# Two kernel tables issued by ScalarE, one embedding tile ahead of the first inner product, one weight split moved

## The chip, the cores and the metric

The kernel runs on one core of one Trainium2 chip. The metric is the device time in microseconds of one execution. The kernel before took 1217.81 us (median of three runs, 1214.92 to 1218.32). All matrix work is float32 done as three products of split halves, so TensorE (PE) is busy almost throughout; the change concerns one stage of about 60 us in the middle, where it is not.

## The reference, cut to what matters

Two layers over 512 positions of 1024 channels. Layer 0 mixes positions with a gated MLP and an attention, layer 1 with a diagonal complex state-space layer. After the mixing, each layer runs a gated feed-forward block and adds a gated embedding:

```python
for i in range(DEPTH):
    h = rms_norm(x, norm_mix[i])
    if i % 2 == 0:
        ...
    else:
        y = s5_mixer(h, ...)                     # 64 groups of 16 channels, 64 complex states each
        g_a, g_b = jnp.split(jax.nn.gelu(y) @ od_w_glu[o], 2, axis=-1)
        x = x + g_a * jax.nn.sigmoid(g_b)
    x = x + conv_ffn(rms_norm(x, norm_ffn[i]), ...)
    gate = jax.nn.sigmoid(rms_norm(x) @ ple_w_gate[i])
    x = x + gate * (p[i] @ ple_w_proj[i])
```

## The kernel before

The activations lie transposed, as eight tiles `x[0]` to `x[7]` of 128 channels by 512 positions. A product `W @ x` takes each weight chunk (128 x 1024 floats, 512 KB) as `raw` from HBM, splits it into a rounded part `whi` (ACT, line 136) and a remainder `wlo` (DVE, line 140), and does three matmuls per 128x128 block: `whi` with the low half of the activations (line 188), `whi` with the high half (189), `wlo` with the high half (190).

`Stream` (called `ws`) hands out the chunks in a fixed order. `n_dma`, `n_prep` and `n_use` count the chunks loaded, split and used; `prep(upto)` splits every chunk below `upto` that isn't split yet, but none at or beyond `limit`; `next()` first splits the chunk it hands out, if that has not been done, and then up to two more. There are four `raw` buffers and three of `whi` and `wlo`. Around the change the order of chunks is: eight of layer 0's gate (`w_gate`), two of layer 1's embedding projection (`w_proj`), sixteen of the GLU (`w_glu`).

The order of the instructions on each engine is that in which the Python code writes them; nothing reorders them. `after(n, fn)` puts a step off to a later `tick()`. `ple(0)` computes the gated embedding of layer 0; `gate(m)` and `add(m)` update `x[m]`, square it (`sq_add`) and write it, regrouped, to HBM (`s5_turn`) for the next stage.

`state_space` is the state-space layer. Its channels go in four rounds `b` = 0 to 3, two tiles each. For a round:

- `inputs(b)` (PE, line 1510) multiplies the regrouped activations `u` with input matrices `wv` into `V`.
- `frame(b)` (DVE, lines 1522 to 1533; one product, line 1526, on POOL) turns `V` by phase tables `tab`, scans along the sequence, and turns back; `states(b)` (DVE, line 1545) writes the states into `sg`.
- `inside(b)` (PE, line 1553) multiplies `u` with the kernel table `tt`, and `outside(b)` (PE, line 1562) adds the states times the output matrices `wo`, both into `Y`; ACT applies GELU to `Y` (line 1566).
- `turn(b)` transposes the result on PE (line 1575), and `done(b)` splits it into `ygh` (ACT, line 1590) and `ygl` (DVE, line 1591).

`tt`, `tab` and `wo` have two buffers each, and `wv` four. `load_kernel(b)` fills a `tt` with eight transfers of 128 KB, each for 16 partitions and in pieces of 512 bytes. All these loads stand in one queue, that of SP; each waits for its buffer to come free, and what stands behind it waits with it. One `tab` buffer, and the `sg` buffers, first hold the split embedding `phl` that `p_proj(w, m, ...)` multiplies by `w_proj` (lines 188 to 190, result `pk`), so `tab` of round 1 and the first write to `sg` wait for the last `p_proj`. `part` multiplies the GLU weights with what is ready of `yg`, and fills PE's time in rounds 2 and 3.

Of the kernel before, what the change touches and what calls it, by code (L numbers as in the profile page):

```python
# [19 lines left out]
P = 128  # L20
# [134 lines left out]
class Kern:  # L155
# [861 lines left out]
    def ple(self, layer, pl):  # L1017
        nc = self.nc
        pp = [pl.tile([P, T], F32, name=f"pp{m}") for m in range(KT)]
        self.after(1 + (layer == 0), self.rms_stat)  # L1020
        self.after(2 + (layer == 0), self.rms_bcast)
        if layer == 0:
            self.p_proj(lambda m, ps: nc.scalar.activation(pp[m], ps, AF.Copy))
        else:
            for m in range(KT):
                nc.sync.dma_start(pp[m], self.pd[m])

        gt = {}

        def gate(m, ps, c=slice(0, T)):  # L1030
            last = layer == 0 and m == KT - 1
            if c.start == 0:
                gt[m] = pl.tile([P, T], F32, name="gt", tag="gt", bufs=4)
            if last:
                add(m - 1)
            t = gt[m]
            nc.vector.tensor_tensor(t[:, c], ps[:, c], self.rB[:, c], ALU.mult)

            def rest():
                nc.scalar.activation(t[:, c], t[:, c], AF.Sigmoid)  # L1040
                if 0 < m < KT - 1 and c.start == 0:
                    add(m - 1)
                if m == KT - 1 or (layer and m == KT - 2):
                    add(m, c)

            self.post.append(rest)
            if m == KT - 1:
                self.run_post()

        def add(m, c=slice(0, T)):  # L1050
            t = gt[m]
            nc.vector.tensor_tensor(t[:, c], t[:, c], pp[m][:, c], ALU.mult)
            nc.vector.tensor_tensor(self.x[m][:, c], self.x[m][:, c], t[:, c], ALU.add)
            if layer == 0:
                if m == KT - 1:
                    self.s5_turn(m - 1, pl)
                self.sq_add(m, self.x[m], m == KT - 1)
                if m != KT - 2:
                    self.s5_turn(m, pl)
            else:  # L1060
                nc.sync.dma_start(self.out[m][:, c], self.x[m][:, c])

        for m in range(KT):
            hi, lo = self.ws.next()
            if layer and m == KT - 1:

                for c in (slice(0, T // 2), slice(T // 2, T)):
                    ps = self.acc()
                    xs = [(h[:, c], l[:, c]) for h, l in self.xh]
                    self.mtile(ps[:, c], hi, lo, range(KT), xs)  # L1070
                    gate(m, ps, c)
                continue
            ps = self.acc()
            self.mtile(ps, hi, lo, range(KT), self.xh)
            lag = 2 if layer and m < 2 else 1
            self.after(lag, lambda m=m, ps=ps: gate(m, ps))
            if layer == 0:
                self.s5_early(m)
            self.tick()
        if layer:  # L1080
            self.flush()
# [309 lines left out]
            self.nc.sync.dma_start(tab.rearrange("p a b -> p (a b)"), self.tabd[b])  # L1391
            self.units["tab", b] = tab[:, 0], tab[:, 1], self.de[b].rearrange("p g j -> p (g j)")

    def load_kernel(self, b):
        if b < 4:
            tt = self.s5a.tile([P, 16, P], F32, name="tt", tag="tt", bufs=2)
            src = self.kd[b].rearrange("(g c) k -> c g k", c=16)
            for i in range(8):
                self.nc.sync.dma_start(tt[i:P:8], src[:, :, P - 16 * i:2 * P - 16 * i])
            self.units["tt", b] = tt  # L1400

    def load_in(self, u):
# [59 lines left out]
    def state_space(self, s5b):  # L1462
        nc, gp, s5a = self.nc, self.gp, self.s5a

        def bank(b, name):
            return self.pp.tile([P, T], F32, name=name, tag=f"bank{b}", bufs=1)
# [4 lines left out]
        def p_proj(w, m, b):  # L1471
            ps = bank(b, "pk")
            o = 2 * (m % 4) * P
            self.mtile(ps, w[0][:, o:], w[1][:, o:], range(2), self.p)
            if m < 6:
                t = gp.tile([P, T], F32, name="pk", tag=("xh0", "xh1", "xh2", "xh3", "xl6", "xl7")[m])
            else:
                t = s5b.tile([P, T], F32, name="pk", tag=("ygh1", "ygl1")[m - 6], bufs=1)
            nc.scalar.activation(t, ps, AF.Copy)
            kept.append(t)  # L1480
# [19 lines left out]
        def inputs(b, b0, tiles=(0, 1)):  # L1500

            if 0 in tiles:
                V[b] = [bank(b0 + r, "V") for r in range(2)]
            vs = V[b]
            for uu in tiles:
                wv = self.units["wv", 2 * b + uu]
                for q in range(4):
                    for r in range(2):
                        for h in range(2):
                            nc.tensor.matmul(vs[r][64 * h:64 * h + 64, (4 * uu + q) * 64:(4 * uu + q + 1) * 64],  # L1510
                                             wv[:, r, q, 64 * h:64 * h + 64], self.ut[2 * b + uu][:, 2 * q + h],
                                             start=True, stop=True)
# [34 lines left out]
        def inside(b, b0):  # L1547

            Y[b] = [bank(b0 + z, "Y") for z in range(2)]
            tt = self.units["tt", b]  # L1550
            for g in range(8):
                for k in range(2):
                    nc.tensor.matmul(Y[b][g // 4][64 * k:64 * k + 64, g % 4 * P:(g % 4 + 1) * P],
                                     self.ut[2 * b + k][:, g], tt[:, 8 * k + g], start=g % 4 == 0, stop=False)
# [49 lines left out]
        w = self.ws.next()  # L1604
# [14 lines left out]
        w = self.ws.next()  # L1619
# [13 lines left out]
        for k in range(4, 8):  # L1633
            scaled(k, rt)
        self.ws.limit = None
        self.ws.prep(self.ws.n_use + 1)
        inside(0, 0)
        self.load_kernel(2)
        p_proj(w, 7, 7)
        inputs(1, 4)  # L1640
        self.load_in(6)
        self.load_in(7)
# [2 lines left out]
        outside(0)  # L1645
        self.load_out(2)
        self.load_out(3)
        self.load_kernel(3)
        for m in (6, 7):
            nc.sync.dma_start(self.pd[m], kept[m])  # L1650
        frame(1)
# [20 lines left out]
        w = self.ws.next()  # L1672
# [14 lines left out]
        w = self.ws.next()  # L1687
# [4 lines left out]
        w = self.ws.next()  # L1692
# [4 lines left out]
        w = self.ws.next()  # L1697
        for m in range(4):
            part(w, 2 * m, m, 4, 6)
        w = self.ws.next()  # L1700
# [14 lines left out]
        w = self.ws.next()  # L1715
# [35 lines left out]
```

## Time and profile before

| | before |
|---|---|
| median of three runs | 1217.81 us (1214.92 to 1218.32) |
| the profiled execution | 1216.31 us, span 1214.4 us |
| TensorE clock granted, mean | 0.995 |
| busy over the span: PE, PE weight loads, DVE, ACT, POOL | 98%, 80%, 65%, 44%, 21% |
| HBM read and written | 131.20 MB, 17.84 MB |

The profiled execution took 1.91 us more than its span. PE's share is an average: it is close to 100% before and after the state-space stage. That stage lies between 651 us (the first `p_proj`) and 725 us of the span; inside it the rows of the timeline, not the averages, tell what waits for what.

### The profile page before, as it was taken

What the parts mean: (1) busy time and instruction counts of PE and PEld (TensorE: products, weight loads), DVE (VectorE), ACT (ScalarE), POOL (GpSimd) and SP (SyncE); (2) the same over time, 40 slices, a digit from 0 to 9 for tenths busy, and PEclk for the clock granted to TensorE, in tenths of its full rate; (3) what the DMA queues carried; (4) which work ended last, traced back from release to release, by engine and by line L of the source; (5) the groups of instructions that cost most, each with busy time, mean ns of one, the idle gap of its engine ahead of it and who ended that gap; (6) DMA issues with size and microseconds to landing.
All of it is one profiled execution on the core that took longest, in us unless ns stands there. A gap on an engine that the chain in (4) does not pass through costs nothing. (4 is left out here: it accounts for less than half of the span.)

```text
span 1214.4 us, 15570 instructions
## 1 busy us (share of the span) xinstructions
PE 1191.8 (98%) x5858; PEld 966.7 (80%) x5858; DVE 784.2 (65%) x1160; ACT 531.5 (44%) x796; POOL 260.4 (21%) x440
## 2 busy tenths in 40 slices
PE   9999999999999999999999789999999999999998
PEld 7887678888888888887888678888888888888787
DVE  5696556599778776775546974449866532456545
ACT  6554664355444333444555224335534421344341
POOL 1652335860960221012302100110000000000110
PEclk9999999999999999999999989999999999999999
DMA  7223124233443545334487952322332333331441
GB/s 253 90 87 140 36 70 139 87 113 104 139 127 103 171 150 163 109 94 145 138 262 206 275 194 86 106 87 87 104 104 87 92 91 99 101 100 54 125 156 70
DMA packets 62314, 150.05 MB, mean 124 GB/s; under 512 B 14408, under 2 KB 23880, under 8 KB 62112
## 3 DMA queue, kind: packets, MB, share of 16 engines
q1 hardware_dynamic: 57504, 135.30, 35.9%
q0 software_dynamic: 4160, 12.90, 3.1%
q8 instruction: 46, 0.75, 0.3%
q10 hardware_dynamic: 576, 0.86, 0.2%
q14 instruction: 28, 0.23, 0.1%
HBM read 131.20 MB, written 17.84 MB: 123 GB/s over the span
## 5 line engine op out<-in xcount | busy, mean ns | idle before, releaser
L140 DVE TENSOR_TENSOR wlo<-raw,whi 128x1024 fp32r<-128x1024 f32 (+3 forms) x207 | 250.0, 1209 | 226.3 <-ACT whi L136 221.2
L136 ACT ACTIVATE whi<-raw 128x1024 fp32r<-128x1024 f32 (+3 forms) x207 | 209.0, 1011 | 354.2 <-PE acc L189 300.0
L188 PE MATMUL acc<-nl,whi 128*128 128x512 f32 x480 | 187.4, 390 | 0.0
L189 PE MATMUL acc<-nh,whi 128*128 128x512 f32 x480 | 187.0, 390 | 0.0
L190 PE MATMUL acc<-nh,wlo 128*128 128x512 f32 x480 | 187.0, 390 | 0.0
L241 POOL TENSOR_TENSOR sqa<-sqa,sqt 128x512 f32<-128x512 f32 x30 | 39.4, 1315 | 492.5 <-ACT sqt L237 492.4
L188 PE MATMUL acc<-xl,whi 128*128 128x512 f32 (+1 forms) x360 | 141.3, 392 | 0.0
L190 PE MATMUL acc<-xh,wlo 128*128 128x512 f32 (+1 forms) x360 | 140.5, 390 | 0.0
L189 PE MATMUL acc<-xh,whi 128*128 128x512 f32 (+1 forms) x360 | 140.5, 390 | 0.0
L188 PE MATMUL acc<-al,whi 128*128 128x512 f32 x352 | 139.2, 395 | 0.4 <-ACT whi L136 0.4
L190 PE MATMUL acc<-ah,wlo 128*128 128x512 f32 x352 | 138.0, 392 | 1.1 <-DVE wlo L140 1.1
L189 PE MATMUL acc<-ah,whi 128*128 128x512 f32 x352 | 137.8, 392 | 0.0
L188 PEld LDWEIGHTS acc<-nl,whi 128*128 128x128 f32 x480 | 90.2, 188 | 19.1 <-issue 0.4
L190 PEld LDWEIGHTS acc<-nh,wlo 128*128 128x128 f32 x480 | 90.1, 188 | 18.7
L189 PEld LDWEIGHTS acc<-nh,whi 128*128 128x128 f32 x480 | 90.2, 188 | 18.5
L925 DVE SCALAR_TENSOR_TENSOR cv<-acc,vecs,cv 128x511 f32<-128x511 f32 x120 | 89.5, 746 | 2.1
L190 PEld LDWEIGHTS acc<-xh,wlo 128*128 128x128 f32 x360 | 67.8, 188 | 15.5
L189 PEld LDWEIGHTS acc<-xh,whi 128*128 128x128 f32 x360 | 67.8, 188 | 15.2
L188 PEld LDWEIGHTS acc<-xl,whi 128*128 128x128 f32 x360 | 67.8, 188 | 15.2
L190 PEld LDWEIGHTS acc<-ah,wlo 128*128 128x128 f32 x352 | 66.1, 188 | 16.5 <-DVE wlo L140 1.9
L188 PEld LDWEIGHTS acc<-al,whi 128*128 128x128 f32 x352 | 66.1, 188 | 16.4 <-ACT whi L136 1.4
L189 PEld LDWEIGHTS acc<-ah,whi 128*128 128x128 f32 x352 | 66.1, 188 | 14.0
(385 smaller groups left out, 1944.0 us busy)
## 6 DMA issues: line engine op xcount, KB each, us to landing
raw<-w_up SPq DMA_DIRECT2D x88, 512.0 KB, 3.5
raw<-w_down SPq DMA_DIRECT2D x26, 512.0 KB, 3.6
raw<-w_in SPq DMA_DIRECT2D x19, 512.0 KB, 3.5
raw<-w_down SPq DMA_DIRECT2D x22, 384.0 KB, 3.1
raw<-w_gate SPq DMA_DIRECT2D x16, 512.0 KB, 3.5
raw<-w_glu SPq DMA_DIRECT2D x16, 512.0 KB, 4.3
x<-xT SPq DMA_DIRECT2D x16, 256.0 KB, 4.5
raw<-w_out SPq DMA_DIRECT2D x8, 512.0 KB, 3.6
```

The source lines that it names most:

```text
L136: k.nc.scalar.activation(hi[:, :n], t[:, :n], AF.Copy)
L140: e.tensor_tensor(lo[:, :n], t[:, :n], hi[:, :n].bitcast(F32), ALU.subtract)
L188: mm(out, whi, xlo, start=start, stop=False)
L189: mm(out, whi, xhi, start=False, stop=False)
L190: mm(out, wlo, xhi, start=False, stop=stop)
L241: (e or (nc.vector if m == KT - 1 else nc.gpsimd)).tensor_tensor(self.sqa, self.sqa, t, ALU.add)
L925: nc.vector.scalar_tensor_tensor(t[:, k:T], h[:, 0:T - k], w[2 - k], t[:, k:T], ALU.mult, ALU.add)
```

## The change

Three edits:

1. `add(7)` in `ple(0)` calls `prep(n_use + 2)` between the regrouping of `x[6]` and the squaring of `x[7]`, with the limit lifted for the call. In `state_space` the call `prep(n_use + 1)` after `states(0)` is removed.
2. The last embedding tile `p_proj(w, 7, 7)` stands ahead of `inside(0)`; it stood behind.
3. The kernel tables of rounds 2 and 3 are issued from ACT's queue; they were issued from SP's.

```diff
@@ ple: add(m), layer 0
                 if m == KT - 1:
                     self.s5_turn(m - 1, pl)
+                    self.ws.limit = None
+                    self.ws.prep(self.ws.n_use + 2)
+                    self.ws.limit = self.ws.n_use + 2
                 self.sq_add(m, self.x[m], m == KT - 1)
@@ load_kernel
-    def load_kernel(self, b):
+    def load_kernel(self, b, q=None):
...
-                self.nc.sync.dma_start(tt[i:P:8], src[:, :, P - 16 * i:2 * P - 16 * i])
+                (q or self.nc.sync).dma_start(tt[i:P:8], src[:, :, P - 16 * i:2 * P - 16 * i])
@@ state_space
         self.ws.limit = None
-        self.ws.prep(self.ws.n_use + 1)
+        p_proj(w, 7, 7)
         inside(0, 0)
-        self.load_kernel(2)
-        p_proj(w, 7, 7)
+        self.load_kernel(2, nc.scalar)
         inputs(1, 4)
...
         self.load_out(3)
-        self.load_kernel(3)
+        self.load_kernel(3, nc.scalar)
```

The changed code has three lines more ahead of `state_space`, so a line of that function that is L1562 before is L1566 in the changed kernel.

What the change does to the order on ACT, from the squaring of the last tile `x_119` to the third round. Before (`xp` is the regrouped tile, `pk` an embedding tile, `kd_87` and `kd_88` are the tables of rounds 2 and 3 in HBM):

```order
L237 ACTIVATE sqt<-x_119 128x512
L1417 ACTIVATE xp<-x_119 128x512
L1479 ACTIVATE pk<-pk 128x512 x7
L136 ACTIVATE whi<-raw 128x1024
L1479 ACTIVATE pk<-pk 128x512
L1566 ACT_TABLE_LOAD
L1566 ACTIVATE y<-Y 128x4x8x16 x2
L1590 ACTIVATE ygh_6202<-Z 128x128x4 x2
L1566 ACTIVATE y<-Y 128x4x8x16 x2
L1590 ACTIVATE ygh_6355<-Z 128x128x4 x2
L136 ACTIVATE whi<-raw 128x1024 x2
```

The same stretch of ACT in the changed kernel:

```order
L237 ACTIVATE sqt<-x_119 128x512
L1421 ACTIVATE xp<-x_119 128x512
L1483 ACTIVATE pk<-pk 128x512 x8
L1403 DMA tt<-kd_87 16x16x128 x8
L1570 ACT_TABLE_LOAD
L1570 ACTIVATE y<-Y 128x4x8x16 x2
L1403 DMA tt<-kd_88 16x16x128 x8
L1594 ACTIVATE ygh_6198<-Z 128x128x4 x2
L1570 ACTIVATE y<-Y 128x4x8x16 x2
L1594 ACTIVATE ygh_6351<-Z 128x128x4 x2
L136 ACTIVATE whi<-raw 128x1024 x3
```

The sixteen table transfers stand around the first GELU, ahead of the first `ygh`. The split of the first GLU chunk has left its place among the `pk`; it does not stand by the squaring, but behind the second round's `ygh`, with the next two.

On DVE, the place where round 1's `frame` begins (`u_5907` is the last tile scaled, `V` what `frame(1)` reads), and the place ahead of round 3's `frame`. Before:

```order
L1496 TENSOR_TENSOR u_5907<-u_5907,rj 128x512
L140 TENSOR_TENSOR wlo<-raw,whi 128x1024
L1522 TENSOR_TENSOR st_6154<-V,tab 128x512
L1523 TENSOR_TENSOR st_6155<-V,tab 128x512
...
L1545 TENSOR_TENSOR sg_5859<-st_6311,st_6307 64x8x63 x2
L140 TENSOR_TENSOR wlo<-raw,whi 128x1024 x2
L1522 TENSOR_TENSOR st_6428<-V,tab 128x512
```

DVE in the changed kernel, from the last update of `x_119` to the reciprocal root `rc` of the summed squares, and then the same two places:

```order
L1053 TENSOR_TENSOR x_119<-x_119,gt 128x512
L254 TENSOR_SCALAR rc<-aux 128x4
...
L1500 TENSOR_TENSOR u_5907<-u_5907,rj 128x512
L1526 TENSOR_TENSOR st_6150<-V,tab 128x512
L1527 TENSOR_TENSOR st_6151<-V,tab 128x512
...
L1549 TENSOR_TENSOR sg_5859<-st_6307,st_6303 64x8x63 x2
L140 TENSOR_TENSOR wlo<-raw,whi 128x1024 x3
L1526 TENSOR_TENSOR st_6428<-V,tab 128x512
```

One `wlo` has moved from ahead of `frame(1)` to ahead of `frame(3)`, where there are now three in a row; between `x_119` and `rc` there is none. On PE only the six matmuls of the last `pk` have changed places with the 32 of `inside(0)`, and on SP the two tables are gone from between the other loads.

## The prediction

> **What bounds the kernel now.** I read the spans and the granted clock first, then busy time by stretch, then the timelines of DVE, PE, SP and ACT through the state-space stage. All times are of the profiled execution of before: 1216.31 us, span 1214.4 us. Its three other runs have a median of 1217.81 (1214.92 to 1218.32). The clock, then engine by engine the busy time of three stretches:
>
> ```profile
> core 0: 1214.4 us, clock 0.995
> ...
> 180.00:640.00 460.00, 459.28 (x2150) 374.56 (x2149) 325.88 (x421) 209.09 (x314) 162.84 (x278) 1.00 0.44 138
> 645.00:725.00 80.00, 67.44 (x699) 55.96 (x697) 66.90 (x91) 27.66 (x40) 10.72 (x10) 0.94 0.77 221
> 725.00:1210.00 485.00, 484.13 (x2150) 397.84 (x2148) 265.71 (x331) 184.07 (x241) 19.48 (x14) 1.00 0.31 97
> ```
>
> PE idles 0.72 us before the state-space stage, 12.56 us inside these 80 us, and 0.87 us behind them. So time can only be won or lost inside. DVE, where it says "<-" what ended an idle time:
>
> ```profile
> 657.24 0.16 DVE L254 TENSOR_SCALAR rc<-aux 128x4 f32<-128x4 f32 x1 [1.87 <-PE aux L245]
> ...
> 671.91 2.79 DVE L1545 TENSOR_TENSOR sg<-st,st 64x504 f32<-64x504 f32 x4
> 674.73 2.50 DVE L1496 TENSOR_TENSOR u<-u,rj 128x512 f32<-128x512 f32 x4
> 677.15 1.22 DVE L140 TENSOR_TENSOR wlo<-raw,whi 128x1024 fp32r<-128x1024 f32 x1
> 678.28 0.69 DVE L1522 TENSOR_TENSOR st<-V,tab 128x512 f32<-128x512 f32 x1
> ...
> 686.62 1.28 DVE L1591 TENSOR_TENSOR ygl<-Z,ygh 128x512 fp32r<-128x512 f32 x2
> 687.93 2.79 DVE L1545 TENSOR_TENSOR sg<-st,st 64x504 f32<-64x504 f32 x4
> ...
> 703.27 2.36 DVE L140 TENSOR_TENSOR wlo<-raw,whi 128x1024 fp32r<-128x1024 f32 x2
> 705.55 0.68 DVE L1522 TENSOR_TENSOR st<-V,tab 128x512 f32<-128x512 f32 x1
> ...
> 715.18 2.79 DVE L1545 TENSOR_TENSOR sg<-st,st 64x504 f32<-64x504 f32 x4
> ```
>
> No row of DVE from 663 to 719 us has an idle note, those shown among them: DVE runs without a gap, and the last `sg` (715.18 + 2.79 = 717.97) sets when PE can finish `outside(3)`. PE (start, duration, line, count, idle before):
>
> ```profile
> 665.56 1.97 PE L1553 MATMUL Y<-tt,u 128*64 128x128 f32 x32
> 667.46 0.50 PE L188 MATMUL pk<-phl,whi 128*128 128x512 f32 x1
> ...
> 674.76 1.75 PE L1562 MATMUL Y<-wo,sg 128*64 128x128 f32 x28 [0.18 <-DVE sg L1545]
> 680.52 3.58 PE L1553 MATMUL Y<-tt,u 128*64 128x128 f32 x32 [4.02 <-DMA wv<-wvd]
> 684.03 1.09 PE L1575 MATMUL Z<-ident,y 128*128 128x128 f32 x8
> ...
> 699.88 0.50 PE L188 MATMUL acc<-ygl,whi 128*128 128x512 f32 x1 [2.60 <-DVE ygl L1591]
> ...
> 705.81 1.97 PE L1562 MATMUL Y<-wo,sg 128*64 128x128 f32 x32
> ...
> 718.03 3.25 PE L1562 MATMUL Y<-wo,sg 128*64 128x128 f32 x28 [0.27 <-DVE sg L1545]
> 721.21 0.58 PE L188 MATMUL acc<-ygl,whi 128*128 128x512 f32 x1
> ```
>
> PE waits 4.02 us before `inside(2)` and 2.60 us before the first GLU `part`; from 721.21 it runs to the end. So the end of the kernel is the start of the row at 721.21 plus constant work. Clock by stretch (PEclk is the column behind the five engines):
>
> ```profile
> 680.50:684.10 3.60, 3.58 (x33) 3.37 (x34) 3.53 (x5) 0.00 (x0) 1.28 (x1) 0.53 1.02 404
> 701.00:704.30 3.30, 3.30 (x10) 2.52 (x9) 3.19 (x5) 0.00 (x0) 0.00 (x0) 0.50 0.06 26
> 717.80:721.20 3.40, 3.17 (x28) 2.85 (x28) 1.40 (x2) 0.60 (x1) 0.00 (x0) 0.53 0.27 54
> ...
> 699.88:715.63 15.75, 15.75 (x88) 12.57 (x88) 15.43 (x21) 3.23 (x5) 1.29 (x1) 0.89 0.69 242
> ```
>
> After a mostly idle stretch PE runs some 3.3 us at half clock: 32 matmuls of `inside(2)` take 3.58 us, 32 of `outside(2)` at 705.81 take 1.97. The third half-clock stretch hits `outside(3)` itself: its 28 matmuls take 3.25 us, the same form at 674.76 takes 1.75. That is 1.5 us on the path.
>
> **The split of the first GLU chunk.** It does not go where the change writes it. When `add(7)` runs, all eight gate chunks are used and nothing more, so `prep(n_use + 2)` asks for the two embedding chunks, which the `next()` of the last gate chunk has split already. The call does nothing, and the gap of 1.87 us before 657.24 stays empty. With the later `prep` removed, the chunk is split by the `next()` ahead of the first `part`: the order of the changed kernel has `whi` behind the second `ygh` and `wlo` behind `states(2)`. So:
>
> - ACT: one instruction of 1.05 us leaves a place where ACT had nothing else (row 666.21 below) and goes to one where ACT is idle too: 0 us. If that cover were gone, 1.05 us.
> - DVE: the row at 677.15 goes, and `frame(1)` starts 678.28 - 677.15 = 1.13 us earlier. It comes back behind 703.24: two take 2.36, three 3.49. At `frame(3)` the sum is 0.
> - PE: before, the first `part` waited only for its PSUM bank (`ygl` of round 1). Now its third matmul needs the moved `wlo`.
>
> **The embedding tile ahead of inside(0).** Six matmuls (1.4 us) and 32 (1.97 us) change places; `inputs(1)` starts when it did, so PE gains and loses nothing. But the tile's input lies in `sg`, which POOL clears before its product of frame 0:
>
> ```profile
> 668.49 0.19 POOL L1625 MEMSET sg<- 128x16 f32 x2 [9.99 <-PE pk L190]
> 668.67 1.47 POOL L1526 TENSOR_TENSOR st<-st,tab 128x512 f32<-128x512 f32 x1
> ```
>
> ```profile
> 669.09 1.59 DVE L1531 TENSOR_TENSOR st<-st,tab 128x512 f32<-128x512 f32 x1
> ...
> 684.80 0.69 DVE L1531 TENSOR_TENSOR st<-st,tab 128x512 f32<-128x512 f32 x1
> ```
>
> POOL's product overlaps DVE's L1531, which takes 1.59 us, where the same line takes 0.69 in round 1, at 684.80, clear of POOL. In the changed order the clearing comes about 2 us earlier, and the product ends before L1531; it will lie on L1529 instead and cost some of it. The loss is 1.59 - 0.69 = 0.9; I take a gain of 0.3, between 0 and 0.9, because most of it comes back at L1529. Together with the split, `frame(1)` starts 1.43 us earlier and ends near 685.2 instead of 686.6.
>
> **The tables.** SP and ACT:
>
> ```profile
> 669.14 0.32 SPq L1391 DMA_DIRECT2D tab<-tabd  x1
> 669.51 5.79 SPq L1399 DMA_DIRECT2D tt<-kd  x8
> 675.39 1.02 SPq L1405 DMA_DIRECT2D wv<-wvd  x2
> ...
> 678.70 9.65 SPq L1399 DMA_DIRECT2D tt<-kd  x8
> ```
>
> ```profile
> tt<-kd SPq DMA_DIRECT2D x2, 128.0 KB, 5.4
> ```
>
> ```profile
> 666.21 1.05 ACT L136 ACTIVATE whi<-raw 128x1024 fp32r<-128x1024 f32 x1
> ...
> 669.77 1.28 ACT L1566 ACT_TABLE_LOAD   x1
> 675.68 0.60 ACT L1566 ACTIVATE y<-Y 128x512 f32<-128x512 f32 x1 [4.63 <-PE Y L1562]
> ...
> 684.73 1.09 ACT L1590 ACTIVATE ygh<-Z 128x512 fp32r<-128x512 f32 x2 [7.55 <-PE Z L1575]
> ```
>
> The first is the queue of SP: a phase table, eight pieces of `tt` for round 2, then `wv` and, at 678.70, eight pieces for round 3. The last piece of round 2 was issued in the window 674.5 to 675.3 and took 5.4 us to land, so about 680.1 to 680.5, just when `inside(2)` starts: that wait, which the chain of waits lays on `wv`, is one for `tt`.
>
> Issued by ACT, they can start when `inside(0)` is done, now at the end of the embedding tile's old place, 669.05: 0.45 us earlier than 669.51. Eight issues at 5.79 / 8 = 0.72 us end at 674.9, the GELU's table load (1.28) at 676.2, the two GELUs at 677.5; before, the second ended at 677.2. So round 2's table costs ACT nothing that anybody waits for: `outside(0)` ends at 676.5 in any case, and PE reads this GELU only behind `inside(2)`. Round 3's eight issues follow, and behind them on ACT is `ygh` of round 0, for which DVE waits with `ygl` and everything after. At 0.72 us each they end at 683.3, at the 9.65 / 8 = 1.21 us of row 678.70 at 687.2. DVE would want `ygl` at 685.2, about 0.6 us behind the first `ygh`; so the stall is 0 to 2.6 us, and between the two, at 0.96, 0.6 us.
>
> The other stall is the table itself. SP, freed of sixteen issues, sends `wv` (two of 512 KB) and the next phase table at 671 to 672 us, as soon as their buffers are free, instead of from 675.39. They now run beside `tt` of round 2. At 404 GB/s (row 680.50) those 1.57 MB are 3.9 us of transfer. If all of it goes ahead of the rest of `tt`, the table lands 3.9 - 0.45 = 3.45 us later, if none, 0.45 us earlier. Before, `ygl` could have run at 684.73 + 0.6 = 685.3, as 0.1 us later than now needed; so this stall is 0 to 3.5 us. I take half of the transfers, 1.95 - 0.45 + 0.1 = 1.6. The stalls run at the same time, so the larger counts: 1.6 us, a middle value, since both queues hold work all the time and no row tells their shares.
>
> The Trainium skill, page "DMA: Bandwidth & Descriptors", section "Issuing engines are not separate DMA queues", speaks against this edit: transfers from different engines run on the same 16 DMA engines and interleave, and a second issuer saves only the issuing time. By that rule the tables come late by their share, as in my sum; if ACT's queue were a lane of its own, the stall would be 0 and the sum 1.6 us lower.
>
> What else stands behind the sixteen issues on SP (output matrices, the last phase table, GLU chunks) only comes earlier. One load comes later: the late split holds its `raw` buffer until 703 instead of 678, and the GLU load that reuses it waits in SP's queue. Its cover is that nobody wants that chunk before 721, and that the output matrices behind it wait for `outside(2)` (705.81 + 1.97 = 707.8) anyway: 0 us. Without the cover it would cost a landing time, 5 us or so.
>
> **PE from the first part on.** `states(2)` ends at 703.24 - 1.43 = 701.8, the moved `wlo` at 703.0. There the third matmul starts; before, the first stood at 699.88. Row 699.88:715.63 is 15.75 us at a clock of 0.89, so 14.0 us at full clock, less two matmuls (0.5): 13.5. The idle time before is over 4 us, so a half-clock stretch follows as in the rows: I take 1.65 us lost (3.3 at 0.50), against 0 and, if it lasts two stretches, 3.3. PE reaches `outside(3)` at 703.0 + 13.5 + 1.65 = 718.2. `sg` is ready at 717.97 - 0.3 = 717.7, so PE no longer waits, comes without an idle stretch, and does `outside(3)` at full clock in 1.9: it ends near 720.1, 1.1 us before 721.21. In words: 1.5 us are won at the clock, 0.4 lost to the later start.
>
> **Sum.** -1.1 + 1.6 = +0.5 us: 1216.31 becomes 1216.8. The profiled execution lies 1.5 us under the median of the runs; all four executions seen have a middle of 1217.06, and 1217.06 + 0.5 is 1217.56, rounded to 1217.5. The extremes without a jam: if PE is never slow, DVE's 717.7 and 1.75 us for the last 28 matmuls end `outside(3)` at 719.45, which is -1.8; and with both bounds against it +3.5 - 1.1 + 1.65 = +4.0. What a measurement can tell is some 0.3%, 3.65 us.
>
> The clock term has a page too: "TensorE: Matmul & The Clock Gate" in the Trainium skill, section "What's actually happening", says that a free-running window of 3413 ns decides, and that an idle one halves the clock. The trace agrees as far as it goes (0.53, 0.50, 0.53 over some 3.4 us each). By that rule a restart late in a window would leave that window too idle as well, and the half clock would last up to a window longer; as an estimate by the page that loses up to 1.7 us more than I took, and the sum would be +2.2.
>
> **Rivals.**
>
> - No stall. The pieces of 512 bytes slip between the big transfers, the table lands by 680, and ACT is through by 684. Then -1.1 to -1.8: 1215.3 to 1216.0. For it: `inside(2)` may start any time up to 680.4 without harm. Against it: DMA is busy through this stretch, and the issues of row 678.70 came 1.21 us apart.
> - ACT jams, and the kernel is slower. If ACT's issues take 1.21 us both times, round 2's end at 678.7, the GELUs at 681.2, round 3's at 690.9, and `ygl` stands at 691.5, 6.3 us late: 6.3 - 1.1 = +5.2, 1222.3. It passes 3.65 us when an issue takes more than about 1.1 us. For it: row 678.70, with other transfers pending, and now there are always some. Against: row 669.51, and ACT's queue has nothing older in it at 669.
> - The split does what the description says, in the gap before 657.24. Then DVE would end 1.43 us sooner, no third `wlo` stands before `frame(3)`, and PE's wait stays 2.6 us: -1.4, or 1215.7. The order speaks against it.
>
> **How the numbers follow.** The forecast (a stall of some 0.5 to 3.5 us) has 0.50, no stall 0.33, the jam 0.13, the split as described 0.02, something else 0.02. No row holds 3.65 us to win, so faster is only scatter: 0.05. Slower is most of the jam (0.10) and some scatter: 0.11. The rest, 0.84, is within 0.3%. The runs of before scatter by 1.7 us about their middle; with the bounds -1.8 and +4.0 and some of the jam that gives 1213.8 to 1221.5.
>
> **What the profile after would show.** No `whi` on ACT and no `wlo` on DVE between 652 and 703 us; three `wlo` ahead of `frame(3)`. `frame(1)` about 1.4 us earlier. PE's first `part` broken after two matmuls for some 4 us, and no wait before `outside(3)`, its 28 matmuls in 1.75 us. DVE's one gap before `ygl` of round 0, ended by ACT. It is wrong if that gap is over 5 us, if DVE also waits at `frame(2)` or later, or if PE waits for a GLU chunk behind 721 us.

## The result and the profile after

The changed kernel takes 1227.08 us (median of 4 runs, 1225.84 to 1228.80) against 1216.37 us for the kernel before (4 runs): ratio 1.009, 95% interval 1.0075 to 1.0105. It is slower by 10.7 us; the forecast was 1217.5, with a range of 1213.8 to 1221.5.

The profiled execution took 1228.80 us, at a lower mean clock than before (0.995):

```profile
core 0: 1227.0 us, clock 0.991
```

In the timeline of the same execution (start, duration, what, idle time before and what ended it), first ACT's queue and ACT, then SP's queue, DVE and PE:

```profile
671.07 15.14 ACTq L1403 DMA_DIRECT2D tt<-kd  x8
686.41 1.20 ACTq L1403 DMA_DIRECT2D tt<-kd  x2
687.53 1.08 ACT L1570 ACTIVATE y<-Y 128x512 f32<-128x512 f32 x2
691.91 5.34 ACTq L1403 DMA_DIRECT2D tt<-kd  x6
697.30 1.09 ACT L1594 ACTIVATE ygh<-Z 128x512 fp32r<-128x512 f32 x2 [8.68 <-DMA tt<-kd]
...
673.96 0.78 SPq L1395 DMA_DIRECT2D tab<-tabd  x1
678.38 0.80 SPq L1415 DMA_DIRECT2D wo<-wod  x2
687.47 0.32 SPq L1395 DMA_DIRECT2D tab<-tabd  x1
687.83 1.02 SPq L125 DMA_DIRECT2D raw<-w_glu  x2
...
664.73 0.69 DVE L1526 TENSOR_TENSOR st<-V,tab 128x512 f32<-128x512 f32 x1 [0.60 <-PE V L1514]
669.22 1.32 DVE L1533 TENSOR_TENSOR st<-st,st 128x512 f32<-128x512 f32 x1
671.84 0.69 DVE L1535 TENSOR_TENSOR st<-st,tab 128x512 f32<-128x512 f32 x1
679.00 0.68 DVE L1526 TENSOR_TENSOR st<-V,tab 128x512 f32<-128x512 f32 x1
697.93 1.29 DVE L1595 TENSOR_TENSOR ygl<-Z,ygh 128x512 fp32r<-128x512 f32 x2 [10.54 <-ACT ygh L1594]
714.54 3.50 DVE L140 TENSOR_TENSOR wlo<-raw,whi 128x1024 fp32r<-128x1024 f32 x3
...
688.53 3.68 PE L1557 MATMUL Y<-tt,u 128*64 128x128 f32 x32 [10.18 <-DMA tt<-kd]
715.82 0.80 PE L190 MATMUL acc<-ygh,wlo 128*128 128x512 f32 x1 [3.34 <-DVE wlo L140]
731.95 1.97 PE L1566 MATMUL Y<-wo,sg 128*64 128x128 f32 x32
```

Read it from the bottom. `outside(3)` ends at 731.95 + 1.97 = 733.92, that is 69.19 us behind the first instruction of `frame(0)` (664.73). Before, the same stretch took 718.03 + 3.25 - 662.62 = 58.66. I call this stretch the stage. It makes the result: the difference is 10.5 us, and behind it both kernels take the same 493.1 us (1227.0 - 733.92 and 1214.4 - 721.28). Ahead of it the two profiled executions differ by 2.1 us, which the last section takes up. Inside it DVE, which ran without a gap, has one of 10.54 us before `ygl` of round 0. It waits for `ygh`, which stands on ACT behind the sixteen table issues. PE waits 10.18 us for the table of round 2. The eight issues of that table, 5.79 us on SP, take 15.14 us on ACT.

The issues are not slow themselves. Six of them, each alone (the fifth to seventh of round 2, the third, fifth and sixth of round 3), and then the issue-to-landing times of four of SP's transfers (the issue at 673.96, the second at 678.38, and the two at 687.83):

```profile
674.95 0.62 ACTq L1403 DMA_DIRECT2D tt<-kd  x1
681.63 0.54 ACTq L1403 DMA_DIRECT2D tt<-kd  x1
685.01 0.54 ACTq L1403 DMA_DIRECT2D tt<-kd  x1
691.91 0.54 ACTq L1403 DMA_DIRECT2D tt<-kd  x1
693.25 0.54 ACTq L1403 DMA_DIRECT2D tt<-kd  x1
695.39 0.54 ACTq L1403 DMA_DIRECT2D tt<-kd  x1
```

```profile
tab<-tabd SPq DMA_DIRECT2D x1, 512.0 KB, 7.7
...
wo<-wod SPq DMA_DIRECT2D x1, 512.0 KB, 6.2
...
raw<-w_glu SPq DMA_DIRECT2D x1, 512.0 KB, 5.4
...
raw<-w_glu SPq DMA_DIRECT2D x1, 512.0 KB, 7.0
```

An issue takes 0.62 or 0.54 us (one of the first five took 1.87). Between them ACT's queue stands still twice in round 2, from 675.57 to 681.63 and from 682.17 to 685.01, which is 8.9 of the 15.14 us; the issuing itself is the other 6.2. It goes on when one of SP's transfers has landed: 673.96 + 7.7 = 681.66, 678.79 + 6.2 = 684.99, 687.83 + 5.4 = 693.2, 688.41 + 7.0 = 695.4 (of the phase table issued at 687.47 the trace has no landing). The built program says why. Every transfer of SP and ACT is given one of eight landing semaphores (counters that a transfer raises when it has landed), `DMAHW0` to `DMAHW7`, in turn, and an issue waits until the transfer that had the same one before has landed. The turn is counted over both queues together. The sixth and seventh piece of round 2 and the third, fifth and sixth of round 3 on ACT, and five loads on SP, with their waits:

```
ACT L1403 DMA tt_6049<-kd2_87 16x16x128 [waits DMAHW2_49]
ACT L1403 DMA tt_6049<-kd2_87 16x16x128 [waits DMAHW5_49]
ACT L1403 DMA tt_6139<-kd3_88 16x16x128 [waits DMAHW1_49]
ACT L1403 DMA tt_6139<-kd3_88 16x16x128 [waits DMAHW3_49]
ACT L1403 DMA tt_6139<-kd3_88 16x16x128 [waits DMAHW4_49]
SP L1395 DMA tab_6114<-tabd2_67 128x1024 [waits DMAHW2_49,DVE_49,Pool_49]
SP L1415 DMA wo_6137<-wod3_80 128x1024 [waits DMAHW5_49,PE_49]
SP L1395 DMA tab_6168<-tabd3_68 128x1024 [waits DMAHW1_49,DMAHW6_49,DVE_49,Pool_49]
SP L125 DMA raw_6208<-w_glu 128x1024 [waits DMAHW3_49]
SP L125 DMA raw_6210<-w_glu 128x1024 [waits DMAHW4_49]
```

Row by row, ACT's pieces hang on SP's phase table, output matrix, next phase table and two GLU chunks, and these wait for buffers that DVE and PE must free first. The Trainium skill, page "Perfetto Trace Analysis", section "DMA Instruction — HWDGE (DVE, Sync)", says that the profile's start of such an instruction is when its semaphores are satisfied; the trace agrees, since a held issue shows 0.54 us and the hold shows in no issue's own row.

### The profile page after: what moved, and what is told of

Same layout as the page of the kernel before. It is cut to its first block, busy times and chain, and to the rows that moved or that the text cites. A ratio compares the mean times of both kernels' runs of the same rounds, so it can differ in the third digit from the quotient of the medians.

```text
span 1227.0 us, 15567 instructions
## 1 busy us (share of the span) xinstructions
PE 1194.2 (97%) x5858; PEld 967.8 (79%) x5858; DVE 784.9 (64%) x1160; ACT 531.3 (43%) x796; POOL 259.5 (21%) x440
```

## The experiments

Two theories. **Sharing:** the tables are late, and ACT's issues slow, because SP's large transfers run on the same DMA engines. **Turn:** ACT's issues are held by the landing semaphores that they share with SP's transfers. All numbers, before the single runs ("eight issues": round 2's table, from first issue to the end of the last; the stage is worked out as above; each ratio is to runs of before in the same rounds, whose medians were 1216.63 for e1 to e4, 1217.22 for e5 to e8 and 1217.14 for e9 and e10):

| kernel | median us (runs) | ratio to before, interval | eight issues us, queue | PE's wait before inside(2) | DVE's gap before ygl 0 | stage |
|---|---|---|---|---|---|---|
| before | 1216.37 (4) | | 5.79 SP | 4.02 | 0 | 58.66 |
| after | 1227.08 (4) | 1.0090, 1.0075 to 1.0105 | 15.14 ACT | 10.18 | 10.54 | 69.19 |
| e1_tables_sp | 1216.02 (11) | 0.9996, 0.9987 to 1.0004 | 5.46 SP | 1.44 | 0 | 58.62 |
| e2_split_old | 1226.43 (5) | 1.0076, 1.0062 to 1.0090 | 16.57 ACT | 11.92 | 10.88 | 68.96 |
| e3_tile_first | 1216.35 (11) | 1.0000, 0.9991 to 1.0008 | 5.91 SP | 1.45 | 0 | 57.59 |
| e4_split_squares | 1213.33 (10) | 0.9974, 0.9964 to 0.9983 | 5.59 SP | 1.23 | 0 | 55.75 |
| e5_sp_later | 1231.69 (4) | 1.0119, 1.0101 to 1.0136 | 18.41 ACT | 18.79 | 14.33 | 72.51 |
| e6_sp_loads_pool | 1227.50 (4) | 1.0091, 1.0076 to 1.0106 | 10.03 ACT | 12.01 | 10.54 | 69.37 |
| e7_tables_pool | 1219.93 (7) | 1.0026, 1.0015 to 1.0037 | 4.55 POOL | 7.43 | 2.33 | 62.48 |
| e8_round3_act | 1217.72 (10) | 1.0007, 0.9997 to 1.0017 | 6.48 SP | 1.79 | 0 | 58.93 |
| e9_act_alone | 1222.62 (5) | 1.0046, 1.0032 to 1.0060 | 6.71 ACT | 9.04 | 5.43 | 63.17 |
| e10_round2_act | 1224.38 (4) | 1.0058, 1.0043 to 1.0073 | 13.29 ACT | 10.98 | 7.11 | 65.63 |

**e1_tables_sp: the change with the tables back on SP.**

```diff
-        self.load_kernel(2, nc.scalar)
+        self.load_kernel(2)
...
-        self.load_kernel(3, nc.scalar)
+        self.load_kernel(3)
```

> The changed kernel with both kernel tables issued from SP again; the late split and the early embedding tile stay. Theory A (the tables on ACT's queue cost everything: their eight pieces crawl while SP sends its big loads, and ACT's GELU and ygh stand behind them): the loss of about 10.7 us goes, and by the working of the prediction without a stall the kernel is -1.0 us against before, ratio 0.998 to 1.001. Rival B (the late split of the first GLU chunk costs it: PE waits for the third wlo and runs at half clock afterwards): still +8 us or more, ratio 1.007 or above.

The 10.7 us are gone; the other two edits together change nothing that can be measured.

**e2_split_old: the change with the split at its old place.**

```diff
         self.ws.limit = None
+        self.ws.prep(self.ws.n_use + 1)
         p_proj(w, 7, 7)
```

(and the call in `add(7)` is out again.)

> The changed kernel with the split of the first GLU chunk at its old place; the tables stay on ACT, the embedding tile stays first. Theory A: still slower by 9 to 12 us, ratio 1.008 to 1.010, ACT's eight issues of round 2's table again take about 15 us, PE waits about 10 us before inside(2). Rival B: back to before within 1.5 us.

Still slow, with a wait of 11.92 and a gap of 10.88 us, like the change's. So, with e1, the tables on ACT are the cause, whatever the split does.

**e3_tile_first: only the embedding tile moved,** the other two edits undone.

```diff
+        p_proj(w, 7, 7)
         inside(0, 0)
         self.load_kernel(2)
-        p_proj(w, 7, 7)
```

> The kernel before with one edit: the last embedding tile ahead of inside(0). POOL's product of frame 0 ends before DVE's L1531. Theory: -0.3 us (0 to -0.9), not to be told from 1.000 by the time; in the trace L1531 of round 0 takes 0.69 us instead of 1.59 and L1529 about 1.3 instead of 0.69. Rival: nothing of it reaches the end, since the first table of round 2 is issued no earlier, 0.0.

```profile
666.94 1.29 DVE L1529 TENSOR_TENSOR st<-st,st 128x512 f32<-128x512 f32 x1
669.53 0.69 DVE L1531 TENSOR_TENSOR st<-st,tab 128x512 f32<-128x512 f32 x1
...
666.86 0.32 SPq L1391 DMA_DIRECT2D tab<-tabd  x1
...
677.50 1.97 PE L1553 MATMUL Y<-tt,u 128*64 128x128 f32 x32 [1.45 <-DMA tt<-kd]
```

The overlap with POOL moves from L1531 (0.69, was 1.59) to L1529 (1.29), as foretold. Not foretold: the phase table of round 1 is issued at 666.86 instead of 669.14, since it waits for the last `p_proj`, and with the table behind it `inside(2)` can start at 677.50 instead of 680.52, at full clock. DVE sets the pace, and the times show no gain (ratio 1.0000). In the one profile the stage is 1.07 us shorter, but 0.77 of that is the clock: the 28 matmuls of `outside(3)` take 2.48 us instead of 3.25.

**e4_split_squares: e1, with the split asked for where the change meant it.**

```diff
-                    self.ws.prep(self.ws.n_use + 2)
+                    self.ws.prep(self.ws.n_use + 3)
```

> Tables on SP, embedding tile first, and the split asked for one chunk further (n_use + 3), so that it does stand between the regrouping of x[6] and the squaring of x[7]. Theory: ACT's whi takes 1.05 us in an idle time of 1.21, DVE's wlo 1.23 us in one of 1.87, nothing behind them moves; frame(1) starts 1.13 + 0.3 us earlier and there are two wlo ahead of frame(3): -1.4 us (-1 to -3), ratio 0.9975 to 0.999. Rival: the table of round 2 still lands as late as in before, DVE then waits for round 0's ygl, and only 0.1 to 0.3 us are left.

```profile
654.84 1.22 DVE L140 TENSOR_TENSOR wlo<-raw,whi 128x1024 fp32r<-128x1024 f32 x1
656.79 0.16 DVE L254 TENSOR_SCALAR rc<-aux 128x4 f32<-128x4 f32 x1 [0.73 <-PE aux L245]
...
716.20 1.75 PE L1566 MATMUL Y<-wo,sg 128*64 128x128 f32 x28 [0.27 <-DVE sg L1549]
```

Now the split fills DVE's gap before `rc` (0.73 left of 1.87), and `outside(3)` runs at full clock. This version beats both kernels: 1213.33 us, 3.3 us below the 1216.63 of before in the same rounds, a little more than the 1 to 3 expected. The clock is not one profile's luck: its mean over the execution is 0.998 in nine of the ten runs, and in one of the 26 of before. Why it comes back is open; PE waits 1.54 us ahead of its last 32 matmuls in both kernels.

**e5_sp_later: SP's input matrices of round 3 and the phase table behind the output matrices.** Between the landing of round 1's phase table (672.3) and the output matrices (issued at 678.05) no large load of SP is in flight.

```diff
-        self.load_in(6)
-        self.load_in(7)
         inside(1, 6)
-        self.load_tab(2)
         outside(0)
         self.load_out(2)
         self.load_out(3)
+        self.load_in(6)
+        self.load_in(7)
+        self.load_tab(2)
```

> The changed kernel, but SP's input matrices for round 3 and the phase table of round 2 are issued behind the output matrices, so behind the wait for outside(0); SP has nothing big in flight while ACT issues round 2's table. Theory A (an ACT issue is held until an older transfer of another queue has landed): round 2's eight issues take 5 to 6.5 us instead of 15.1, inside(2) waits under 3 us instead of 10.2, round 3's eight still crawl (8 us or more) since SP's loads are now beside them, the gap of DVE before the first ygl is 2 to 7 us, 1218 to 1223 us. Theory B (issuing such a table is slow on ACT, about 1.9 us a piece whatever SP does): 15 us again, 1226 to 1229 us. Theory C (SP's transfers only take the bandwidth): the issues still take 0.7 us each, and the table lands in time.

All three theories missed: the eight issues took longer, not shorter. ACT's queue, a window of the whole core, and SP's load:

```profile
670.75 18.41 ACTq L1403 DMA_DIRECT2D tt<-kd  x8
...
684.29 0.54 ACTq L1403 DMA_DIRECT2D tt<-kd  x1
...
678.89 0.90 SPq L1409 DMA_DIRECT2D wv<-wvd  x2
```

```profile
676.80:678.00 1.20, 1.20 (x24) 0.98 (x18) 1.20 (x3) 0.00 (x0) 0.00 (x0) 1.00 0.00 0
```

```profile
wv<-wvd SPq DMA_DIRECT2D x1, 512.0 KB, 5.4
```

Five pieces went out at the usual pace, 3.7 us in all. From 676.80 to 678.00 the DMA engines are idle (share 0.00, 0 GB/s), and ACT still does not issue the sixth. It comes at 684.29, when the input matrix that SP issued at 678.89 has landed (678.89 + 5.4). Nothing is shared at 677, so this is not contention: the piece waits for a load that SP has not issued yet. This is where I formed the theory of the turn.

**e6_sp_loads_pool: the input matrices, the phase table and the output matrices of round 2 on POOL's queue.**

```diff
-        self.load_in(6)
+        self.load_in(6, nc.gpsimd)
...
-        self.load_out(3)
+        self.load_out(3, nc.gpsimd)
```

> The changed kernel, but the loads that stand between the two tables (input matrices of round 3, phase table and output matrices of round 2) are issued by POOL; ACT still issues the tables. Theory A1 (the queues of SP and ACT hold each other up, whatever the bytes): ACT's sixteen issues take 0.6 to 0.8 us each, 11 us in all, DVE's gap before the first ygl is under 3 us, 1216 to 1220 us. Theory A2 (the sixteen DMA engines, filled with big transfers of whatever queue, hold the small pieces up): ACT's issues crawl as before, 13 us or more for the first eight, 1224 us or more. Theory B (ACT issues slowly by itself): the same as A2, but no issue ends where a big transfer lands.

```profile
668.87 10.03 ACTq L1403 DMA_DIRECT2D tt<-kd  x8
681.69 13.32 ACTq L1403 DMA_DIRECT2D tt<-kd  x8
...
685.22 0.32 SPq L1395 DMA_DIRECT2D tab<-tabd  x1
...
689.85 0.54 ACTq L1403 DMA_DIRECT2D tt<-kd  x1
```

As slow as the change, so by itself it spoke for sharing, though the first eight (10.03 us) lie between the two cases. Piece by piece it does not: transfers of POOL have eight semaphores of their own in the built program (`DMASW0` to `DMASW7`), but the next phase table and two GLU chunks stayed on SP, and the third piece of round 3 goes out at 689.85, when the phase table issued at 685.22 lands (4.6 us). In round 2 ACT now stands behind itself: the fourth piece has the semaphore of the first and goes out at 674.54, when the first (668.87) has landed, 5.6 us after its issue.

**e7_tables_pool: both tables on POOL.**

```diff
-        self.load_kernel(2, nc.scalar)
+        self.load_kernel(2, nc.gpsimd)
...
-        self.load_kernel(3, nc.scalar)
+        self.load_kernel(3, nc.gpsimd)
```

> The changed kernel, but both tables are issued by POOL, so that no ygh or GELU of ACT stands behind them. If the cost is ACT blocked behind its own issues, and the table itself would be in time: inside(2) waits under 3 us, no gap on DVE before ygl, 1215 to 1219 us. If the table is late whoever issues it beside SP's loads: inside(2) waits 6 us or more, and the time is 1222 us or more with ACT free. POOL's product of frame(1) stands behind both tables' issues on POOL; if those are held, DVE waits in frame(1), and that wait shows instead.

```profile
669.08 4.55 POOL L1403 DMA_DIRECT2D tt<-kd  x8 [1.35 <-PE Y L1557]
...
683.52 3.68 PE L1557 MATMUL Y<-tt,u 128*64 128x128 f32 x32 [7.43 <-DMA tt<-kd]
```

```profile
tt<-kd POOLq DMA_DIRECT2D x8, 128.0 KB, 7.8
tab<-tabd SPq DMA_DIRECT2D x1, 512.0 KB, 12.7
```

Between the expected cases. Here nothing holds the issues of round 2's table (4.55 us for eight) and ACT is free: what is left is sharing. A piece takes 7.8 us to land instead of 5.4, SP's phase table 12.7, and PE waits 7.43 us for the table (1.44 in e1). Round 3's issues are held, each until POOL's own piece eight places ahead has landed, and POOL's product of `frame(1)` behind them stretches DVE's L1536 from 0.68 to 2.17 us; but DVE then still waits 2.33 us for `ygh`, so this does not set the pace. That costs 3.9 us of the stage (62.48 against 58.62 in e1).

**e8_round3_act: round 2's table on SP, round 3's on ACT.**

```diff
-        self.load_kernel(2, nc.scalar)
+        self.load_kernel(2)
```

> The changed kernel with round 2's table back on SP and round 3's alone on ACT. If each of the tables costs by itself: ACT's eight issues start after the second GELU (about 677) beside SP's own loads, take 9 to 15 us, the first ygh comes at 687 to 692 instead of 685, DVE gap 2 to 7 us, 1218 to 1223 us. If the first table alone does the harm (its lateness at inside(2) and its delay of the GELUs): DVE gap under 1 us, 1214 to 1217 us.

Eight issues on ACT from 677.86 to 685.60 took 7.74 us, and `ygh` followed at 685.65, just in time: DVE has no gap. The time is 0.7 us above the range of the second case. Round 3's table costs next to nothing when round 2's is on time.

**e9_act_alone: e6, and the remaining transfers of the stretch on POOL too,** so that the same bytes move, and the turn of the eight holds, beside ACT's pieces, only loads that SP issued ahead of them (`ws.q` is the queue that the chunk loads take).

```diff
-            nc.sync.dma_start(self.pd[m], kept[m])
+            nc.gpsimd.dma_start(self.pd[m], kept[m])
...
-        self.load_tab(3)
+        self.load_tab(3, nc.gpsimd)
...
+        self.ws.q = nc.gpsimd
         self.ws.dma(self.ws.n_use + 3)
+        self.ws.q = None
```

> Both tables on ACT as in the changed kernel, but every other transfer of that stretch (input matrices of round 3, phase tables of rounds 2 and 3, output matrices of round 2, the two embedding tiles written out, two GLU chunks) is issued by POOL, whose landing semaphores are its own eight. Theory S (the transfers of SP and ACT share eight landing semaphores in one rotation; an issue waits until the transfer eight places ahead of it in that rotation has landed, and ACT is held by SP's transfers through it): now only ACT's own pieces stand in that rotation, so the first eight issues take 5.3 to 8 us instead of 15.1, the second eight follow the landings of the first, DVE's gap before the first ygl is 1 to 4 us, and the time is 1217 to 1222 us: what stays is the table landing late beside POOL's big transfers, as in the kernel with both tables on POOL (1219.9). Theory H (the DMA engines or ACT's own issuing are slow when big transfers run beside): the first eight 10 us or more, the gap 8 us or more, 1225 us or more, as with part of these loads on POOL (1227.5).

```profile
tt<-kd ACTq DMA_DIRECT2D x8, 128.0 KB, 8.6
```

```profile
670.73 6.71 ACTq L1404 DMA_DIRECT2D tt<-kd  x8
678.15 1.20 ACTq L1404 DMA_DIRECT2D tt<-kd  x2
679.68 7.74 ACTq L1404 DMA_DIRECT2D tt<-kd  x6
...
692.43 0.69 DVE L1596 TENSOR_TENSOR ygl<-Z,ygh 128x512 fp32r<-128x512 f32 x1 [5.43 <-ACT ygh L1595]
```

The turn it is: 6.71 us instead of 10.03 in e6, and the stage 6.2 us shorter, with the same engine issuing. The gap is 1.4 us over the expected 4, and the time 0.6 us over the 1222: ACT's second eight still wait for its own first eight to land, beside POOL's loads. A piece of the first eight takes 8.6 us to land (the first line): with the issuers exchanged, small pieces beside large loads are as late as in e7, so that lateness is not POOL's way of issuing.

**e10_round2_act: round 2's table on ACT, round 3's on SP.**

```diff
-        self.load_kernel(3, nc.scalar)
+        self.load_kernel(3)
```

> The changed kernel with round 2's table alone on ACT, round 3's on SP; the counterpart of the kernel with round 3's alone on ACT (1217.7). Theory S: the sixth to eighth piece of round 2 stand in the rotation behind SP's phase table and output matrices, and are held until these land at about 681 to 685 us; so the table is whole near 688, inside(2) waits 8 to 10 us, the GELUs and the first ygh stand behind the issues, DVE's gap is 5 to 9 us, 1221 to 1226 us: most of the cost is in this table, and round 3's adds the rest. If the two tables' costs only come together (one alone costs 1 us, as round 3's did): 1216 to 1219 us.

```profile
668.85 13.29 ACTq L1403 DMA_DIRECT2D tt<-kd  x8
...
687.10 3.68 PE L1557 MATMUL Y<-tt,u 128*64 128x128 f32 x32 [10.98 <-DMA tt<-kd]
...
692.27 1.29 DVE L1595 TENSOR_TENSOR ygl<-Z,ygh 128x512 fp32r<-128x512 f32 x2 [7.11 <-ACT ygh L1594]
```

Time and gap as the turn foretold; PE's wait is 1.0 us longer, and the pieces went out by 682, 3 us earlier than expected. Round 2's table alone makes 7.0 of the 10.6 us of stage that separate the change from e1; round 3's costs the rest only behind it.

In sum, by the stage: 58.62 with the tables on SP; 62.48 with sharing alone (POOL); 63.17 with ACT held by its own pieces; 69.19 with SP's loads in ACT's turn. So sharing is some 3.9 us of the loss, the turn 6.7. The split into terms rests on kernels in which the order of other loads moves a little too; that ACT is held by SP's landings is shown by e5 and e9 and by the times of the single issues.

## Why the prediction was wrong

- **The step that failed** is the price of an issue on ACT, "0.72 us each", with 1.21 us as its upper bound. ACT took 15.14 us for eight, 1.89 each, because its issues were held by SP's landings; so `ygh` came late and the stall of DVE was 10.54 us, where the sum had 0 to 3.5. The gap of over 5 us that the prediction named as a sign of being wrong is there. I had read the 9.65 us of row 678.70 as eight slower issues. They were the same hold: on SP too a piece waits for the landing of the transfer eight places ahead. In before, four of the eight start at 681.15, 682.51, 683.71 and 685.03, and the two `wv`, the `tab` and the first `wo` issued from 675.39 on landed at 681.1, 682.5, 683.7 and 685.0. On SP it did no harm, since the waiting pieces were round 3's. A bound taken from a row whose mechanism was not looked at is no bound. The waits stood in the built program, and I read only its order.
- **The jam rival** had the right place (`ygh` behind the issues on ACT), at a chance of 0.13 and with +5.2 us. Its price came from the same 1.21 us; it was +10.7.
- **The table's lateness**, "0 to 3.5 us", was right for sharing alone: in e7 the last piece lands 20.8 us behind the start of `frame(0)`, before 17.5, so 3.3 us later, near the upper end and not at the half that I took. In the change itself, where ACT is held, it was wrong: `inside(2)`, which waits for the table, starts 23.80 us behind `frame(0)` (688.53 - 664.73) instead of 17.90 (680.52 - 662.62), 5.9 us later. The rule of the Trainium skill, page "DMA: Bandwidth & Descriptors", section "Issuing engines are not separate DMA queues", that transfers of all issuers interleave on the same engines, agrees with e7. What it does not cover is the hold, which is of the program and not of the DMA engines.
- **The split**: right. The call does nothing, three `wlo` stand at 714.54, and from 652 us to there no `wlo` is seen. The rival "as described" was right in kind and too small: I priced it at -1.4; e4 is 2.9 us of stage below e1. I left out that `outside(3)` gets its full clock back there as well (1.75 against 3.25 in before, 1.5 us).
- **The embedding tile**: right. Together with the split, `frame(1)` starts 14.27 us behind `frame(0)` (679.00 - 664.73) instead of 15.66; I said 1.43 us earlier, it was 1.39. POOL's product now lies on L1533 (1.32 us), and L1535 is down to 0.69. That `tab` of round 1, and with it round 2's table on SP, would come earlier (e3) is not in the prediction.
- **PE from the first part on**, "-1.1 us": right in each step but one size. The third matmul waits for `wlo`, and `outside(3)` comes without a wait and at full clock. But the half clock lasted longer than the 3.3 us taken:

```profile
715.80:722.10 6.30, 6.28 (x17) 4.75 (x17) 6.23 (x8) 0.00 (x0) 0.74 (x1) 0.59 0.75 247
```

  6.30 us at 0.59 lose 2.6 us, not 1.65. In the profile of e1, which has this term and no table on ACT, the stage is 58.62 against 58.66: no gain. The estimate by the Trainium skill, page "TensorE: Matmul & The Clock Gate", section "What's actually happening" (up to a window longer, up to 1.7 us more lost), covers it: 0.9 us more was lost.

## What to carry to other kernels

Before a transfer is moved to another engine's queue, look up what its issue waits for in the built program, landing semaphores included: an issue on a compute engine blocks the compute behind it, and where semaphores are handed out in turn over two queues, it can hang on a load that the other queue has not even issued. Keep many small pieces on a queue that nobody's arithmetic stands in, or on one with semaphores of its own; the second still shares the DMA engines (62.48 us of stage on POOL here, 58.62 on SP). And when an edit is meant to fill a gap, see that it does something there: one number (`n_use + 3` for `n_use + 2`) made the difference between no gain that can be measured (e1) and 3.3 us (e4).

## What the runs showed of the hardware that was not expected

- Small and large transfers that run side by side both take longer: in e7 the 128 KB pieces took 7.8 us to land instead of 5.4, and a 512 KB phase table 12.7 us, where the one at 669.14 in before took 3.5.
- The profiled executions fall into two groups, whose `frame(0)` starts near 662.5 or near 664.5 us. That of before is in the first, that of after in the second. The 2 us arise at the start, where 4 us hold 19 matmuls before and 11 after, each row with a granted clock of 1.00:

```profile
7.00:11.00 4.00, 4.00 (x19) 3.30 (x19) 2.92 (x5) 3.22 (x5) 0.00 (x0) 1.00 1.03 400
```

```profile
7.00:11.00 4.00, 4.00 (x11) 3.13 (x10) 3.06 (x5) 3.20 (x5) 0.00 (x0) 1.00 1.04 410
```

  The first row is of before, the second of after. PE ran slowly there at a clock that reads full: in after a matmul takes 0.63 us until 10.84 us, as in the half-clock stretch behind 715.82, and 0.39 from 11.18 on. So the record of the clock does not seem to hold for the start; what decides how long it lasts was not tried. It is why stages are compared here from `frame(0)` on, and not by the whole time of one execution.
